# One set of tiles for both phases of a hybrid encoder layer: later weights split in the third block, first block's pooling done later, norm ahead of the fold

## The chip, the core and the metric

The kernel runs on one core of a Trainium2 chip, whose engines are named as in the profile: PE multiplies matrices (PEld loads its stationary operand), DVE and ACT do the work on vectors, POOL does a little arithmetic and issues the stores, and SP issues the loads. The metric is the device time of one execution in microseconds (us), from launch to end.

## The reference: what is computed

One encoder layer is applied to two groups, 512 and 2048 tokens of 1024 channels, with the same weights, in f32. Cut to what matters:

```
h = rmsnorm(x, norm_pre)
pool_u, pool_g, q, k, v, attn_g, merge = split(h @ w_in)        # w_in: 1024 x 6656
pooled = mean of pool_u over 2, 4, 8 or 16 neighbours - pool_u  # by channel group
pb = (pooled by group @ w_pool_group) * pool_scale * silu(pool_g)
ab = windowed_attention(rope(q), rope(k), v, sink) * silu(attn_g)
m = sigmoid(merge_p) * (pb @ w_pool_proj) + sigmoid(merge_a) * (ab @ w_attn_proj)
y = x + rmsnorm(m @ w_out, norm_post)
```

Attention sees a band of 128 tokens to either side; 16 heads share 4 heads of keys and values.

## The kernel before, in words

**Precision.** Each f32 operand is split into a high and a low part (`hi_lo`: a copy to the reduced format on ACT, a subtraction on DVE), and a product is three matmuls (`mm3`): high by high, high by low, low by high. So every weight that PE uses costs ACT one copy and DVE one subtraction, unless it was split before and lies split in memory.

**Phase 1** computes the input projection, for tokens in three blocks (768, 896 and 896 tokens), with all the normed tokens of a block held in `arena` as seven operands (B11, T2, B21, T1, T3, B22, T4). The 26 pairs of weight units of a block go through a scheme of seven products (M1, M6, M2, M5, M7, M3, M4, in this order) in place of eight; the sums of weights that it needs (S1 to S4) are formed in the first block (`sums`) and kept in memory for the other two. After its products a pair is finished on DVE and ACT by a `Post`: rotary embedding (`Rope`), gates (`Gate`, `Silu`), values transposed on PE (`Values.tr_steps`), or pooling (`Pool`: running sums over neighbours, a gate, the result stored as `pb`). The two halves U2 and U4 that a pair keeps until M7 and M4 lie in tiles `u`.

The pooling's group weights are folded into its part of the input projection first (`fold`: 32 steps of six matmuls, in items of four steps; an item loads three pieces of weights, `w_pool_group` and two of `wu_t`, into tiles with tag `u`, and splits them). Ahead of the first block the sums of squares of its tokens are taken (`stats_sum`), turned into the norm's factor, spread over the partitions by PE (`prep_r`, tile `rbc`), and the seven operands are formed (`first_operands`), on DVE above all.

Extra work is put beside the products by `hooks[(block, pair, step)]`: the next block's statistics, norm and operands, and the transposes of the values. One block's pairs 0 and 1, and its last two, run interleaved.

**Phase 2** goes over five blocks of 512 tokens: `pp` (pooling branch by `w_pp`), attention in groups of 128 queries by four heads, `ap` (attention branch by `w_ap`), and `out_phase` (by `w_out`, the second norm, the residual). A grid of slots sets which steps of attention stand between which steps of `pp` and `ap`. Here `wsplit` loads a piece of weights at its first use, splits it and stores it split; later uses load it split. `out_phase` has two halves of 512 channels with four accumulators each; when one is full, `evac` squares it on ACT, multiplies it by the norm's gain on DVE, and in the second half scales and adds.

**What sets the order.** PE's order is that of the code. Each other engine's order is set by the framework's scheduler when the program is built; an engine works in that order and waits at each instruction. Tiles with one tag share a fixed number of buffers (`z` 6, `u` 4, `w` 7, `R` 3); an instruction that writes a new tile waits until an old one is no longer read, and a tile that is stored is free when the store has landed. Phase 1 and phase 2 take their own tiles from two pools, `p1` and `p2`, of which the second is opened when the first is closed. `run` loads weights ahead of the steps by 7 tiles in phase 1 and by 5 in phase 2.

## Time and profile before

| | us |
|---|---|
| median of 3 runs | 2493.63 (2488.38 to 2495.53) |
| the profiled execution | 2490.91 |
| its span, first to last instruction | 2489.1 |
| PE busy in it | 2340.3 |
| DVE busy | 1775.7 |
| ACT busy | 1158.1 |

Reading it: the profiled execution lies 2.7 us below the median, and 1.8 us of it lie outside the span. PE's matmuls overlap each other in the trace, so that its busy time says when it was not idle. The granted clock of PE is 1.00 at 2.4 GHz and 0.50 at 1.2 GHz; a mean between them says how much of a stretch was spent at each.

### The profile page before, as it was taken

How to read it: one execution, taken by the hardware profiler on the slowest of the kernel's cores; microseconds unless marked ns; L12 is line 12 of the kernel's file. 1: busy time of each engine (PE TensorE's matmuls, PEld its weight loads, DVE VectorE, ACT ScalarE, POOL GpSimd, SP SyncE). 2: the span in 40 equal slices, each digit the busy share in tenths (PEclk: the TensorE clock that was granted, in tenths of full speed). 3: DMA queues.
4: the chain of work that ended last, by engine and by line, in shares of the span. 5: the costliest groups of instructions: out<-in, count | busy, mean ns of one | idle time of the engine just before them, and what ended most of it. 6: DMA issues, size and time to landing. Idle time of an engine off the chain costs nothing.

```text
span 2489.1 us, 34194 instructions
## 1 busy us (share of the span) xinstructions
PE 2340.3 (94%) x11668; PEld 2074.6 (83%) x11668; DVE 1775.7 (71%) x3370; ACT 1158.1 (47%) x2477; POOL 418.8 (17%) x897
## 2 busy tenths in 40 slices
PE   4799999989999999899999969999999999999998
PEld 4799999978898989798988858778788788878877
DVE  4888889866667777656667658887689488578632
ACT  5444433544443335333333446765466366456411
POOL 2332222112102110301011011112110110011011
PEclk8899999999999999999999989999999999999999
DMA  7676667665556647534444397889778787877774
GB/s 276 201 254 214 219 250 256 206 236 196 177 184 224 250 157 261 207 134 170 156 156 170 120 342 264 273 288 339 260 252 259 277 271 250 285 236 241 275 266 165
DMA packets 180847, 573.55 MB, mean 230 GB/s; under 512 B 25280, under 2 KB 32704, under 8 KB 170688
## 3 DMA queue, kind: packets, MB, share of 16 engines
q1 hardware_dynamic: 139408, 397.00, 48.0%
q0 software_dynamic: 41264, 174.36, 18.3%
q8 instruction: 92, 1.51, 0.2%
q14 instruction: 83, 0.68, 0.1%
HBM read 396.94 MB, written 174.33 MB: 230 GB/s over the span
## 4 chain that ended last, share of the span: by engine, by line
PE 57%; DVE 9%; DMA 6%; issue 4%; ACT 3%; POOL 1%; POOLq 0%; SPq 0%; ACTq 0%; DVEq 0%
PE ps_s L115 8%; PE ps_s L117 8%; PE ps_s L116 8%; PE ps_g L115 7%; PE ps_g L116 7%; PE ps_g L117 7%; PE ps_t L928 3%; PE ps_o L941 2%; DVE ps_s L904 1%; PE ps_o L940 1%; PE ps_s L900 1%; PE ps_s L901 1%; DMA h<-t 1%; DMA h<-ab 1%; DVE pt L85 1%
## 5 line engine op out<-in xcount | busy, mean ns | idle before, releaser
L115 PE MATMUL ps_s<-arena,w 128*128 128x448 f32 (+1 forms) x1512 | 547.4, 362 | 36.0 <-DVE u L381 20.7
L117 PE MATMUL ps_s<-arena,w 128*128 128x448 f32 (+1 forms) x1512 | 542.3, 359 | 0.0
L116 PE MATMUL ps_s<-arena,w 128*128 128x448 f32 (+1 forms) x1512 | 542.3, 359 | 0.0
L115 PE MATMUL ps_g<-arena,w 128*128 128x512 f32 (+2 forms) x1264 | 493.8, 391 | 22.7 <-ACT w L84 11.5
L116 PE MATMUL ps_g<-arena,w 128*128 128x512 f32 (+2 forms) x1264 | 479.9, 380 | 1.0 <-DVE arena L85 0.9
L117 PE MATMUL ps_g<-arena,w 128*128 128x512 f32 (+2 forms) x1264 | 478.6, 379 | 0.0
L84 ACT CAST w<-Q 128x512 fp32r<-128x512 f32 x312 | 192.8, 621 | 391.2 <-PE ps_s L117 335.4
L115 PEld LDWEIGHTS ps_s<-arena,w 128*128 128x128 f32 x1512 | 286.7, 190 | 63.2 <-DVE u L381 28.5
L117 PEld LDWEIGHTS ps_s<-arena,w 128*128 128x128 f32 x1512 | 286.4, 189 | 17.0 <-DVE w L85 0.4
L116 PEld LDWEIGHTS ps_s<-arena,w 128*128 128x128 f32 x1512 | 286.6, 190 | 16.1
L115 PEld LDWEIGHTS ps_g<-arena,w 128*128 128x128 f32 x1264 | 240.7, 190 | 44.6 <-ACT w L84 11.9
L117 PEld LDWEIGHTS ps_g<-arena,w 128*128 128x128 f32 x1264 | 240.6, 190 | 35.9 <-DVE w L85 0.2
L116 PEld LDWEIGHTS ps_g<-arena,w 128*128 128x128 f32 x1264 | 241.2, 191 | 21.9 <-DVE arena L85 2.0
L85 DVE TENSOR_TENSOR w<-Q,w 128x512 fp32r<-128x512 f32 x312 | 214.0, 688 | 31.3 <-ACT w L84 20.7
L906 ACT ACTIVATE P<-ps_s,nm 128x384 f32<-128x384 f32 (+1 forms) x320 | 179.6, 562 | 105.5 <-DVE nm L904 103.1
L85 DVE TENSOR_TENSOR w<-R,w 128x512 fp32r<-128x512 f32 x234 | 160.6, 687 | 86.7 <-ACT w L84 84.0
L84 ACT CAST w<-R 128x512 fp32r<-128x512 f32 x234 | 145.1, 621 | 139.3 <-PE ps_s L117 116.4
L904 DVE CUSTOM_DVE_ANT_0 ps_s<-ps_s,mask,nsink 128x384 f32<-128x384 f32 (+1 forms) x320 | 188.7, 593 | 14.6 <-PE ps_s L901 12.5
L85 DVE TENSOR_TENSOR pt<-ps_t,pt 128x512 fp32r<-128x512 f32 x224 | 153.6, 687 | 13.7 <-ACT pt L84 11.2
L84 ACT CAST pt<-ps_t 128x512 fp32r<-128x512 f32 x224 | 130.3, 583 | 53.0 <-PE ps_t L928 51.6
L928 PE MATMUL ps_t<-ident,P 128*128 128x128 f32 x896 | 141.0, 277 | 13.4 <-DVE P L915 7.3
L361 DVE TENSOR_TENSOR z<-ps_s,u 128x448 f32<-128x448 f32 (+1 forms) x144 | 86.3, 600 | 86.7 <-PE ps_s L117 82.7
(196 smaller groups left out, 3651.0 us busy)
## 6 DMA issues: line engine op xcount, KB each, us to landing
Q<-sw SPq DMA_DIRECT2D x52, 1024.0 KB, 5.1
R<-in_w_h SPq DMA_DIRECT2D x54, 768.0 KB, 6.1
w<-swpw_pp SPq DMA_DIRECT2D x64, 512.0 KB, 4.4
w<-swpw_ap SPq DMA_DIRECT2D x64, 512.0 KB, 4.5
w<-swpw_out SPq DMA_DIRECT2D x56, 512.0 KB, 4.6
sw<-Q POOLq DMA_DIRECT2D x26, 1024.0 KB, 6.3
z<-in_x SPq DMA_DIRECT2D x40, 512.0 KB, 6.0
arena<-q SPq DMA_DIRECT2D x20, 1024.0 KB, 7.5
```

The lines of the kernel that those rows point to most:

```text
L84: A.copy(hi, src)
L85: V.tensor_sub(lo, src, hi.bitcast(F32))
L115: T.matmul(o, lhsT=xs[0], rhs=ys[0], start=start, stop=False, skip_group_check=more)
L116: T.matmul(o, lhsT=xs[0], rhs=ys[1], start=False, stop=False, skip_group_check=more)
L117: T.matmul(o, lhsT=xs[1], rhs=ys[0], start=False, stop=stop, skip_group_check=more)
L361: V.tensor_add(dst, acc[:, c], t[:, c])
L900: T.matmul(s, lhsT=q, rhs=st["kh"][:, kc], start=True, stop=False)
L901: T.matmul(s, lhsT=q, rhs=st["kl"][:, kc], start=False, stop=True)
L904: V.tensor_tensor_reduce(s, s, mask[:, kb0 * 128:kb1 * 128], -1.0, nsink[:, H:H + 1], ALU.add, ALU.min, nm[:, h:h + 1])
L906: A.activation(P[:, 0:nk], s, AF.Exp, bias=nm[:, h:h + 1], scale=-1.0, accum_out=l[:, h:h + 1])
L928: T.transpose(tp[:, h * 128:(h + 1) * 128], pr[h][:, i * 128:(i + 1) * 128], cst["ident"])
L941: T.matmul(o, lhsT=v, rhs=pts[i][:, 1, :], start=False, stop=i == kb1 - kb0 - 1)
```

## The change

- **One set of tiles.** The pools `p1` and `p2` are gone. Phase 2 takes the tiles of phase 1 under their tags: its gates the `u` tiles, the attention's probabilities an `R` tile for four heads, their transposes a `Q` tile for two, the norm's gain the `A21` tiles, `out_phase`'s products the `rope`, `rbc` and `s` tiles. The squares are written to that product's tile rather than to one of their own. Both phases are one program, `run(phase1() + phase2(), 7)`. The two operand sets of phase 2 change places in `arena`.
- **Later weights.** All 48 pieces of `w_pp`, `w_ap` and `w_out` are loaded, split and stored in the third block of phase 1, 24 times 1024 columns, at hooks beside its pairs. Phase 2 loads them split only.
- **First block's pooling.** In the first block `Pool.finish` stores the two raw tiles (`rawu`, `rawg`). Eight hooks, four in the second and four in the third block, load them again (`again`) and pool (`later`).
- **Norm ahead of the fold.** The six squares stand together at the start, the norm's factor is taken at once (`rstd`), and `prep_r` follows 4 steps of the fold in place of 16; the operands' other parts follow 8 steps. Five of the eight items of the fold now stand between the first two pairs' products, where three stood.
- **Smaller moves.** The four steps that transpose the values stand wider apart; the next block's statistics and norm come some pairs earlier; in `out_phase` the last two pieces of weights are taken accumulator by accumulator; the first attention group follows 24 steps of `pp` in place of 9, and its loads are issued after 8.

```diff
-TILES_H, TILES = 7, 5
+TILES = 7
...
+    def utile():
+        return sb.tile([128, 512], F32, tag="u", bufs=4, name="u")
...
-    def prep_r(p1, s):
+    def rstd(s):
         t0, t1 = BLOCKS[s][0] // 128, BLOCKS[s][1] // 128
         n, ssq = t1 - t0, ssqs[s]
         G.tensor_scalar(ssq[:, 0:n], ssq[:, 0:n], 1.0 / D, EPS, op0=ALU.mult, op1=ALU.add)
         G.tensor_tensor(rcol[:, t0:t1], ssq[:, 0:n], mhalf[:, 0:n], ALU.pow)
-        rbc[s] = p1.tile([128, 896], F32, tag="rbc", bufs=1, name="rbc")
+
+    def prep_r(s):
+        t0, t1 = BLOCKS[s][0] // 128, BLOCKS[s][1] // 128
+        rbc[s] = row_tile()
...
+            if s > 0:
+                self.silu()
+                V.tensor_copy(gcarry[:, f, :], g[:, W:W + 8])
+                self.pool()
+                return
...
+            store(rawu[f], u[:, 0:n])
+            store(rawg[f], g[:, 8:8 + W])
+
+        def again(self):
+            self.z = [ztile(), ztile()]
+            nc.sync.dma_start(self.z[0][:, 0:self.n], rawu[self.f])
+            nc.sync.dma_start(self.z[1][:, 8:8 + self.W], rawg[self.f])
+
+        def later(self):
+            self.silu()
+            self.pool()
...
         def first():
...
-            xs = stats_load(0, range(3))
+            stats_sum(0, range(n0), stats_load(0, range(n0)))
+            rstd(0)
             fold0.load()
-            xs += stats_load(0, range(3, n0))
-            stats_sum(0, range(n0), xs)
             next(forming)
+            pairs[0].raw()
+            next(forming)
+            pairs[1].raw()
...
+        def beside(s, i, load, form, j=0):
+            box = {}
+            hook(s, i, j, lambda: box.update(x=load()))
+            hook(s, i, j + 3, lambda: form(box["x"]))
...
-            for j, f in enumerate(posts[NPAIR * s + 1].tr_steps()):
-                hook(s, 2, 2 + j, f)
+            for (i, j), f in zip(((2, 2), (2, 4), (3, 0), (3, 3)), posts[NPAIR * s + 1].tr_steps()):
+                hook(s, i, j, f)
...
+        first_pools = [x for x in posts[:NPAIR] if isinstance(x, Pool)]
+        for x, (s, i) in zip(first_pools, ((1, 14), (1, 15), (1, 20), (1, 22), (2, 5), (2, 7), (2, 11), (2, 13))):
+            beside(s, i, x.again, lambda _, x=x: x.later())
+        places = [i for i in range(2, NPAIR - 2) if i not in (5, 7, 11, 13)]
+        places = sorted((places + places)[:24])
+        for u in range(24):
+            i = places[u]
+            beside(2, i, lambda u=u: split_load(u), lambda x: split_form(*x), 2 if u and places[u - 1] == i else 0)
...
         prog.append((None, first))
-        prog += fs[0:16]
+        prog += fs[0:4]
         prog.append((None, second))
-        prog += fs[16:20]
+        prog += fs[4:8]
         prog.append((None, third))
-        fs = fs[20:]
+        prog += fs[8:12]
+        fs = fs[12:]
...
+    def split_form(z, dsts):
+        hi, lo = ztile(F32R), z.bitcast(F32R)
+        hi_lo(hi, lo, z)
+        for j, d in enumerate(dsts):
+            for e, t in enumerate((hi, lo)):
+                store(d[:, e, :], t[:, j * 512:(j + 1) * 512])
...
-    SETS = [(region(o, 8, 512), region(o + 4096, 8, 512)) for o in (0, 8192)]
+    SETS = [(region(o, 8, 512), region(o + 4096, 8, 512)) for o in (8192, 0)]
...
-        def wsplit(key, src):
-
+        def weights(key):
             w = wtile()
-            if key in swp:
-                move(w, swp[key])
-                return w
-            raw = p2.tile([128, 512], F32, tag="wr", bufs=3, name="wr")
-            nc.sync.dma_start(raw, src)
-            hi_lo(w[:, 0, :], w[:, 1, :], raw)
-            swp[key] = scratch("swp" + key, [128, 2, 512])
-            store(swp[key], w)
+            move(w, swp[key])
             return w
...
-                A.activation(junk, acc, AF.Square, accum_out=so[:, i:i + 1])
-                o = p2.tile([128, 512], F32, tag="og", bufs=4, name="og")
-                V.tensor_mul(o, acc, cst["gpost"][:, half * 512:(half + 1) * 512])
+                A.activation(o, acc, AF.Square, accum_out=so[:, i:i + 1])
+                V.tensor_mul(o, acc, cst["gpost"][half])
...
-                order = [(u, t) for t in range(4) for u in range(NKT)] if late else [(u, t) for u in range(NKT) for t in range(4)]
+                lead = 0 if late else NKT - 2
+                order = [(u, t) for u in range(lead) for t in range(4)] + [(u, t) for t in range(4) for u in range(lead, NKT)]
...
-                prog += first[:9]
-                fill = at(first[9:], pp_puts(1, 0)) + at(pp(1, 0), ap_puts(0, 1), PUTS0) + ap(0, 1, 0)
+                prog += first[:8] + [(None, lambda: fetch_kv(0, 0))] + first[8:24]
+                fill = at(first[24:], pp_puts(1, 0)) + at(pp(1, 0), ap_puts(0, 1), PUTS0) + ap(0, 1, 0)
...
-        with tc.tile_pool(name="p1", bufs=1) as p1:
-            run(phase1(p1), TILES_H)
-        with tc.tile_pool(name="p2", bufs=1) as p2:
-            run(phase2(p2), TILES)
+        run(phase1() + phase2(), TILES)
```

ACT's order at the start: of before, the part around the spread of the norm's factor (`rbc`); `h` are the fold's results, `w<-R` the first pairs' weights.

```order
L84 CAST w<-R 128x512
L211 COPY rbc<-ps_t 128x512
L211 COPY rbc<-ps_t 128x256
L84 CAST w<-R 128x512
L171 COPY h<-ps_t 128x512
L84 CAST arena<-z 128x384 x2
L171 COPY h<-ps_t 128x512
```

And of the change, from ACT's first work on; `w<-u` are the fold's weights, `arena` the first block's operands.

```order
L222 ACTIVATE z,ssq<-z 128x1024 x6
L105 CAST w<-u 128x512 x3
L197 COPY h<-ps_t 128x512 x2
L240 COPY rbc<-ps_t 128x512
L240 COPY rbc<-ps_t 128x256
L105 CAST arena<-z 128x384 x4
L105 CAST arena<-R 128x384 x4
L105 CAST arena<-z 128x384 x4
L105 CAST w<-u 128x512 x4
```

The factor is spread after one item of the fold rather than after four, and the weights of the fold's second item are now split behind twelve copies of operands.

DVE's order beside the first two pairs: of before, the last item of the fold (`raw`) and the two U4 halves (`u`), with buffer numbers.

```order
L85 TENSOR_TENSOR w_721<-raw_719,w_721 128x512
L85 TENSOR_TENSOR w_726<-raw_724,w_726 128x512
L85 TENSOR_TENSOR w_731<-raw_729,w_731 128x512
...
L389 TENSOR_TENSOR u_839<-ps_s_643,s_555 128x384
...
L389 TENSOR_TENSOR u_856<-ps_s_658,s_570 128x384
```

And of the change; `z_797` and `z_812` are the sums behind M7, which are the last to read the U4 halves `u_889` and `u_903`.

```order
L419 TENSOR_TENSOR u_903<-ps_s_702,s_614 128x384
L391 TENSOR_TENSOR z_797<-ps_s_968,u_889 128x384
L391 TENSOR_TENSOR z_812<-ps_o_985,u_903 128x384
L106 TENSOR_TENSOR w_949<-u_947,w_949 128x512
L106 TENSOR_TENSOR w_954<-u_952,w_954 128x512
L106 TENSOR_TENSOR w_959<-u_957,w_959 128x512
```

The fold's last item stood ahead of the U4 halves and now stands behind M7's sums; its three loads use the buffers of `u_889`, `u_903` and, once more, of `u_889`.

SP's order at the boundary of the phases: of before, from the first loads of attention on (`q`, `k`, `v`); `wr` is the first piece of `w_pp`, still to be split.

```order
L75 DMA arena<-q_114 128x4x512
L75 DMA arena<-k 64x512 x4
L696 DMA mask<-in_mask 128x384
L701 DMA gpost<-in_norm_post 128x1024
L75 DMA arena<-v 128x512
L717 DMA wr<-in_w_pp 128x512 x3
```

And of the change; `w<-w_pp` are pieces that are split already.

```order
L96 DMA w<-w_pp_0_137 128x1024
L828 DMA h<-pb_211 128x512
L96 DMA w<-w_pp_1_138 128x1024
L823 DMA u<-gp_201 128x512
L96 DMA w<-w_pp_0_139 128x1024
L966 DMA z<-sl_185 128x512
L96 DMA w<-w_pp_1_140 128x1024
L96 DMA arena<-q_131 128x4x512
L96 DMA w<-w_pp_0_141 128x1024
```

Four pieces of weights now stand ahead of attention's first load, where all of them stood behind it.

DVE's order at the end of `out_phase`: of before, from the first half's last products to the second half's (`og`; the sums `z<-og,ss,z` need the norm's factor `ss`).

```order
L812 TENSOR_TENSOR og<-ps_t,gpost 128x512 x2
...
L826 SCALAR_TENSOR_TENSOR z<-og,ss,z 128x512 x2
L812 TENSOR_TENSOR og<-ps_g,gpost 128x512 x2
L826 SCALAR_TENSOR_TENSOR z<-og,ss,z 128x512 x2
```

And of the change.

```order
L901 TENSOR_TENSOR s<-ps_g,A_12662 128x512
L915 SCALAR_TENSOR_TENSOR z<-rope,ss,z 128x512
L915 SCALAR_TENSOR_TENSOR z<-s,ss,z 128x512
L901 TENSOR_TENSOR s<-ps_g,A_12662 128x512
```

The product that frees the first accumulator `ps_g` stood behind two sums that wait for the norm's factor, and now stands ahead of them.

## Rows read from the trace of the kernel before

**Rows 1.** Page, busy time of each engine (share of the span), instructions.

```profile
PE 2340.3 (94%) x11668; PEld 2074.6 (83%) x11668; DVE 1775.7 (71%) x3370; ACT 1158.1 (47%) x2477; POOL 418.8 (17%) x897
```

**Rows 2.** Windows: length; PE, PEld, DVE, ACT, POOL busy; clock, DMA share, GB/s.

```profile
0.00:124.50 124.50, 77.41 (x439) 72.58 (x439) 85.91 (x146) 63.53 (x119) 35.83 (x59) 0.88 0.68 239
124.50:503.00 378.50, 358.74 (x2001) 353.28 (x1999) 319.82 (x542) 168.04 (x297) 95.21 (x198) 0.99 0.66 234
580.00:970.00 390.00, 384.35 (x1884) 352.56 (x1883) 275.05 (x417) 165.50 (x280) 51.12 (x97) 1.00 0.58 204
1046.00:1426.00 380.00, 376.31 (x1839) 344.47 (x1839) 252.13 (x383) 148.54 (x245) 46.61 (x93) 1.00 0.43 151
1426.00:1500.00 74.00, 50.89 (x224) 40.84 (x223) 38.71 (x96) 35.19 (x88) 14.15 (x30) 0.84 0.94 338
1500.00:1757.00 257.00, 247.47 (x1219) 202.75 (x1218) 206.57 (x504) 161.62 (x423) 51.53 (x119) 0.99 0.84 286
```

**Rows 3.** PE's waits: for whom, us in total, times, longest us.

```profile
PE ps_t L115 <- ACT w L84: 39.8, 6, 17.3
PE ps_s L115 <- DVE u L381: 20.7, 17, 2.9
PE ps_t L497 <- DVE z L85: 11.9, 5, 2.7
...
PE ps_g L115 <- DVE og L812: 9.8, 4, 2.5
```

**Rows 4.** Timeline of the start: start, us, instruction [idle before <-releaser].

```profile
42.93 0.86 ACT L211 COPY rbc<-ps_t 128x512 f32<-128x512 f32 x2
...
66.89 0.33 SPq L151 DMA_DIRECT2D raw<-in_w_pool_group  x1
...
69.63 0.62 ACT L84 CAST w<-raw 128x512 fp32r<-128x512 f32 x1
...
71.52 0.58 PE L115 MATMUL ps_t<-w 128*128 128x256 f32 x1 [17.27 <-ACT w L84]
```

**Rows 5.** Groups by shape, to 1430 us: busy us, mean ns | idle before.

```profile
L85 DVE TENSOR_TENSOR w<-Q,w 128x512 fp32r<-128x512 f32 x312 | 214.0, 688 | 31.3 <-ACT w L84 20.7
...
L551 DVE TENSOR_TENSOR z<-z 128x904 f32<-128x904 f32 x10 | 10.9, 1092 | 0.0
...
L85 DVE TENSOR_TENSOR arena<-z,arena 128x384 fp32r<-128x384 f32 x14 | 7.4, 550 | 0.7 <-ACT arena L84 0.7
...
L215 DVE SCALAR_TENSOR_TENSOR z<-z,gpre,rbc 128x768 f32<-128x768 f32 x6 | 6.0, 1012 | 0.0
```

**Rows 6.** Windows, columns as in rows 2: one item of the fold and more.

```profile
80.60:83.50 2.90, 2.90 (x26) 2.90 (x25) 2.85 (x8) 1.10 (x2) 0.31 (x1) 1.00 0.42 79
```

**Rows 7.** Timeline, PE behind a pooling of the first block.

```profile
392.72 0.69 PE L115 MATMUL ps_s<-arena,w 128*128 128x384 f32 x1 [2.89 <-DVE u L381]
```

**Rows 8.** Timeline: PE's transposes of values; windows: the clock after another.

```profile
546.37 0.88 PE L497 MATMUL ps_t<-ident,z 128*128 128x128 f32 x3 [2.72 <-DVE z L85]
...
1020.50:1027.20 6.70, 6.12 (x18) 5.30 (x17) 2.45 (x6) 1.64 (x4) 1.43 (x2) 0.50 0.59 196
```

**Rows 9.** Timeline at the boundary of the phases.

```profile
1433.81 2.29 SPq L717 DMA_DIRECT2D wr<-in_w_pp  x3
...
1441.05 0.80 PE L115 MATMUL ps_g<-arena,w 128*128 128x512 f32 x1 [11.47 <-ACT w L84]
```

**Rows 10.** Timeline at the end of `out_phase`; windows: the clock after it.

```profile
1752.86 1.27 DVE L812 TENSOR_TENSOR og<-ps_g,gpost 128x512 f32<-128x512 f32 x2
...
1753.59 0.50 PE L115 MATMUL ps_g<-arena,w 128*128 128x512 f32 x1 [2.47 <-DVE og L812]
...
1754.40:1757.70 3.30, 3.30 (x9) 2.61 (x8) 3.30 (x6) 0.00 (x0) 1.16 (x2) 0.50 0.43 171
```

**Rows 11.** Timeline: ACT and then PE, second block's start.

```profile
567.63 0.94 ACT L84 CAST z<-z 128x896 fp32r<-128x896 f32 x1 [4.42 <-DMA v<-z]
...
573.71 0.74 PE L115 MATMUL ps_s<-arena,w 128*128 128x448 f32 x1 [3.02 <-DVE u L389]
```

More of the change, by code (lines that the diff above doesn't have):

```diff
@@ L142, in run, with fold @@
             f()
-    def fold(p1):
+    def fold():
         steps = []
         def raw_split(src):
-            raw = p1.tile([128, 512], F32, tag="u", bufs=4, name="raw")
+            raw = utile()
             nc.sync.dma_start(raw, src)
@@ L319, in raw @@
                 return
-            self.R = self.p1.tile([128, 1536], F32, tag="R", bufs=NR, name="R")
+            self.R = rtile()
             for c0, c1, src in self.srcs:
@@ L387, in f @@
                 elif r == "M5":
-                    st["U4"] = pair.p1.tile([128, 512], F32, tag="u", bufs=4, name="u")[:, 0:w]
+                    st["U4"] = utile()[:, 0:w]
                     V.tensor_add(st["U4"], acc, st["s"])
@@ L725, in unit @@
             for half in range(2):
-                it = Item(lambda half=half: wsplit(f"{name}{u}_{half}", a[name][u][:, half * 512:(half + 1) * 512]))
+                it = Item(lambda half=half: weights((name, u, half)))
                 for i in range(4):
@@ L837, in make @@
                 def make(u, half=half, late=late):
[L838 removed]
+                    key = "w_out", half, u
                     if not late:
[L840 removed]
+                        return weights(key)
                     w = SETS[1 - mt]
```

149 lines of the change are left out of this document (96 added, 53 removed).

## The prediction, written before the changed kernel was timed

> **What bounds the kernel now.** I read the page first: PE is busy for 2340 us of 2489, DVE for 71%, ACT for half [rows 1]. PE's work stays the same, instruction for instruction, so only PE's 149 us of idle time and the time that it spends at half its clock can be won. Next the windows, cut by stage [rows 2]: the start is idle for 47 us of 124.5 at a mean clock of 0.88; the first block for 19.8 of 378.5; the second and third, behind their first pairs, for only 5.7 and 3.7; the boundary of the phases for 23.1 of 74 at 0.84; the first part of phase 2 for 9.5 of 257. Then PE's waits [rows 3], which name causes: 39.8 us for the fold's weights, 20.7 for U2 (`u L381`), 11.9 for DVE at the transposes of values, 9.8 at the first accumulator behind `out_phase`. In the windows a wait of some 2.5 us or more is followed by a stretch at clock 0.50: 3.3 us of busy PE at half rate, which at full rate had taken half, so 1.7 us on top of the wait [rows 10]; after the transposes of the third block 6.7 us [rows 8].
>
> **The change, part by part.** The sum is made against the profiled execution's 2490.9 us; the median is 2.7 above it.
>
> *End of `out_phase`.* DVE frees `ps_g` at the end of two products at 1752.86, behind sums that wait for the norm, and PE starts at 1753.59 after 2.47 us [rows 10]. In the new order that product stands first. The first accumulator is also full earlier: the last two pieces go accumulator by accumulator, six matmuls each, so three accumulators, 18 matmuls of about 0.2 us (1219 in 247 us [rows 2]), follow the first: 3.7 us in which ACT's square and DVE's product (0.6 to 0.7 us each, the second now behind the first since they write one tile) are hidden. If that cover went, the old 2.5 us would return. Four waits of 2.45 us go [rows 3], and the half-rate stretches behind three of them, 1.7 us each (one is in [rows 10]): **minus 15**.
>
> *The boundary.* SP issues the first `w_pp` at 1433.8, behind attention's loads, and PE stands for 11.5 us until ACT has split it [rows 9]. Afterwards four split pieces stand ahead of the first load of attention; they need neither ACT nor DVE, and the operand set 1, now in B11, T2 and B21, is free after M2, with 96 matmuls of 0.2 us still to come, 19 us before phase 1 ends. The load of `q` still blocks SP, but only until M3 of the last pair has been read; the four pieces give PE 48 matmuls, 10 us, and the keys, values and later pieces have 24 steps (72 matmuls, 15 us) to land where 9 steps stood. Of the stage 23.1 us are idle; a clock of 0.84 makes 24 of 74 us at half rate, and if half of them were busy, 6 more are lost [rows 2]. Of these 29 I leave 3: **minus 26**. Bounds: minus 13 (only the 11.5 and its clock) to minus 29.
>
> *Transposes of values.* A step needs a PSUM tile that DVE must have emptied; with two steps apart in place of one, DVE has 5 us. All 11.9 us of waits [rows 3] and some 6 us of half rate behind them (the longest stretch costs 3.1, half of 6.12 [rows 8]) could go, 18. But the third and fourth step now fall where the pair before finishes a `Rope`, and the values hold two `z` tiles longer: **minus 14**, bounds minus 18 to 0.
>
> *First block's pooling.* A pooling is 4 to 7 instructions of DVE of about 1 us [rows 5] (776 columns in the first block, so 0.97 as an estimate between 768 and 904), 44 us for eight. They leave the first block, where DVE is busy for 84%, and make it 73%. At 71% the second block idles 5.7 us of 390 [rows 2]; so the first should fall from 19.8 to about 8: **minus 12**. The wait of 2.89 us behind such a pooling is one of them [rows 7].
>
> *What the other blocks get.* The second block gets four short poolings, 18 us: DVE 71 to 75%, **plus 3**. The third gets 26 us of poolings and the splits: 48 times 0.688 us, 33 us [rows 5], as 24 instructions of twice the length (estimate 1.3 us). DVE goes from 66% to 82%. Near 84% the first block lost 20 us; but it also formed sums there, which the third does not: from 3.7 to 15, **plus 11**. ACT's 48 copies of 0.62 us [rows 4], 30 us, lie beside 148 of 380, POOL's 96 more stores beside 47 of 380 [rows 2]. Bounds: 0, if all of it fits between PE's needs, to 39, if each of 32 insertions costs the usual wait for `u L381`, 1.2 us (20.7 over 17 [rows 3]).
>
> *Phase 2's first part.* The same 33 us of DVE leave it, from 80 to 67%; of its 9.5 us of idle time 2.5 are `out_phase`'s: **minus 4**, bounds minus 7 to 0.
>
> *The start.* The factor `rbc` is ready at 43.8 us, the fold's sixth item runs at 71.52 after 17.3 us of waiting [rows 4]. Now six loads of 0.5 MB come first, at 239 GB/s [rows 2] 13 us; with 8 us for the factor, one item at half rate and the copies, `rbc` is there at about 21. But in between DVE has 58 instructions to do before the fold's fourth item: 8 norms of 1.01, 16 of 512 columns of 0.69, 34 of 384 of 0.55 [rows 5], 38 us, and ACT splits the fold's second item only behind twelve copies that follow those norms. So the fourth item runs at 59, 12 us earlier, with two items fewer done: 48 matmuls, 5.4 us [rows 6]. Net minus 7. Against it stands the eighth item. Its first two loads need the buffers of the U4 halves, so they wait for M7's sums, and its third needs the first's: load to copy takes 2.7 us [rows 4], twice, with 1.3 for split and subtraction between; PE has only this item ahead. That is 6 us, plus 1.7 at half rate. **Plus or minus 0**, bounds minus 7 to plus 10.
>
> The prefetch by 7 tiles of 7 makes SP wait for PE one piece longer; behind it stand the loads of gates and operands, needed 8 steps (24 matmuls, 5 us) later: nothing, and at worst what little of those loads sticks out of 5 us. The pools' boundary itself costs only what the boundary's term holds.
>
> Sum: -15 - 26 - 14 - 12 + 3 + 11 - 4 + 0 = -57, so 2434 on the profile's scale; with the median somewhat above it I say 2435.
>
> **A rule weighed.** In the third block the DMA engines are busy for 0.43 of the time at 151 GB/s, in the first part of phase 2 for 0.84, with PE busy for 96% [rows 2]. The moved weights and tiles add some 42 MB in 380 us, 110 GB/s, and bring 0.43 to about 0.74, below a share that PE has been seen to bear. The Trainium skill, page "Trainium Kernel Development and Optimization", section Key Constraints, says that the DMAs of all issuing engines run on the same 16 engines and interleave; by that the third block's loads and stores all get slower with the new traffic, which speaks against the move. The trace agrees that the engines are shared: at a share of 0.84 PE still waits little, so by the row it costs nothing, and by the rule alone, transfers longer by two thirds, it would feed the rival below.
>
> **The rivals.**
> - *Slower: `z` tiles run out in the third block.* A split holds two of the six `z` tiles until its four stores have landed, a pooling up to four. That ACT waits 4.4 us for a store of a `z` tile and PE then 3.0 us does occur [rows 11]; with 1.7 at half rate 4.7 us. Were it so at each of 32 insertions, it costs 150 in place of 11: 2574. It decides from 2.5 us per insertion (57 + 11 + 8 over 32) on. Against it: pairs of the third block hold no operands being formed, and a pooling now takes two working tiles, not up to five.
> - *The insertions cost a usual wait each*, 39 in place of 11: 2463.
> - *The boundary only changes its wait*: the split pieces wait behind `q` and the operands behind DVE's last sums, 13 of 26 stay: 2448. This is also the case in which the one set of tiles does not do its work.
> - *The start gains*: the eighth item's stall is covered and DVE forms sooner, 12 to 15 us: 2421.
>
> **How the numbers follow.** Chances: the forecast 0.62, its own range 2412 to 2456 (the bounds of boundary and transposes at one end, of the start and the insertions in part at the other); insertions dear 0.13; boundary 0.08; start 0.11; slower 0.06. The range 2402 to 2472 takes in all but the slower case and the tails of the others. What a measurement of this kernel can tell from no change is about 0.3%, 7.5 us, so 2486 to 2501 is "same": the upper tail of the dear insertions and the near end of the slower case, 0.03; slower 0.04; faster 0.93.
>
> **What would show it.** Right: no wait of PE for `ps_g` behind `out_phase`; PE crosses the boundary with under 5 us idle; DVE near 73% in the first block and 82% in the third; the eighth item of the fold waits some 6 us behind M7. Wrong: ACT or DVE waiting for stores of `z` tiles at many pairs of the third block, or PE idle for over 20 us there; PE still waiting 10 us at the boundary; a start whose fourth item runs much later than 59 us.

## The result: 2.6% slower, and where the time went

The changed kernel takes 2554.64 us (median of 4 runs, 2552.34 to 2564.07) against 2491.88 for the kernel before; the ratio is 1.0259 (95% interval 1.0228 to 1.029). The profiled execution has a span of 2562.3 us, 73.2 more than that of before, and lies 9.4 us above its own median; the sums below are made against these two spans, so some 10 us of them belong to that execution and not to the change.

The page's busy times of the changed kernel, to be held against [rows 1]:

```profile
PE 2361.5 (92%) x11668; PEld 2099.0 (82%) x11668; DVE 1778.3 (69%) x3346; ACT 1156.8 (45%) x2461; POOL 446.3 (17%) x961
```

PE has the same 11668 matmuls and hardly more busy time: the loss is idle time and clock. The windows by stage, columns as in [rows 2]: the start, the first block, the second and third from pair 2 on (pairs are counted from 0), the boundary up to the 96th matmul of phase 2's projections, the first part of phase 2. They begin and end by work done and so not at the places of [rows 2], whose windows of the second and third block begin behind pair 3.

```profile
0.00:112.20 112.20, 69.22 (x366) 65.32 (x367) 69.15 (x120) 57.34 (x107) 26.85 (x41) 0.82 0.64 232
112.20:494.20 382.00, 364.53 (x2036) 361.35 (x2036) 300.09 (x514) 167.09 (x302) 86.80 (x163) 0.98 0.72 250
529.00:989.60 460.60, 428.01 (x2038) 388.73 (x2037) 319.10 (x479) 182.13 (x307) 80.26 (x166) 0.97 0.57 200
1025.30:1517.60 492.30, 429.89 (x2030) 390.11 (x2029) 332.11 (x484) 191.53 (x305) 128.52 (x262) 0.94 0.65 229
1517.60:1547.50 29.90, 27.65 (x122) 22.43 (x122) 8.48 (x24) 7.37 (x20) 2.75 (x7) 0.94 1.03 377
1547.50:1822.70 275.20, 260.83 (x1296) 215.94 (x1295) 206.19 (x520) 161.36 (x435) 29.41 (x88) 0.98 0.77 254
```

The kernel before, second and third block between the same pairs:

```profile
530.40:964.50 434.10, 419.77 (x2038) 383.46 (x2037) 303.85 (x458) 179.47 (x304) 70.87 (x134) 0.99 0.57 202
999.30:1429.20 429.90, 417.98 (x2030) 381.25 (x2030) 283.79 (x429) 166.26 (x276) 68.30 (x134) 0.99 0.46 159
```

In the third block PE is idle for 62.4 us at a clock of 0.94, where before it was idle for 11.9 at 0.99; the second idles 32.6 in place of 14.3. The boundary idles 2.3 us; before, it took 60.3 us up to the same projection matmul and idled 20.3. PE's waits, columns as in [rows 3]:

```profile
PE ps_s L141 <- DVE z L391: 74.1, 17, 17.2
PE ps_t L141 <- ACT w L105: 41.2, 7, 13.9
PE ps_s L141 <- DVE u L411: 28.4, 14, 4.7
PE ps_t L1019 <- DVE Q L106: 19.5, 8, 5.0
```

The same two waits in the kernel before, where attention's transposes are called `pt`:

```profile
PE ps_s L115 <- DVE z L361: 7.3, 5, 2.9
PE ps_t L928 <- DVE pt L85: 5.9, 6, 2.8
```

The first line has grown tenfold: 17 waits of up to 17.2 us for DVE's sum into a pair's `z` tile (L391). The 9.8 us for `og` [rows 3] are gone; the waits for attention's transposes (`Q`) went from 5.9 to 19.5 us.

Since PE's order is the same but for small moves, both traces can be divided by work done: at the first matmul of each pair in phase 1, and at equal counts of projection matmuls in phase 2. The differences of those stretches (after less before, us) add up to the 73:

| stretch | after less before |
|---|---|
| start, pairs 0 and 1 of the first block | +3.2 |
| first block: pairs 2 and 3; the others | +13.0; -15.8 |
| second block: pairs 2 and 3; the others | +5.7; +20.8 |
| third block: pairs 2 and 3; 4, 6, 9, 15, 22; the other pairs | +28.9; +32.4; +1.2 |
| pairs 0 and 1 of the second and third block | -0.9 |
| boundary and first part of phase 2 | -16.5 |
| five output parts and the stretch ahead of the last; the three stretches of attention between the other four | -11.9; +13.2 |

What happens at a bad pair shows in the timeline of the third block's pair 2 (start, us, instruction, idle before and what ended it):

```profile
1043.71 0.78 POOL L99 DMA_DIRECT2D v<-z  x1 [4.19 <-DVE z L106]
1050.20 0.73 POOL L99 DMA_DIRECT2D v<-z  x1 [5.71 <-issue]
1052.78 1.04 ACT L105 CAST z<-z 128x1024 fp32r<-128x1024 f32 x1 [9.23 <-DMA v<-z]
1053.86 1.23 DVE L106 TENSOR_TENSOR z<-z 128x1024 fp32r<-128x1024 f32 x1 [9.85 <-ACT z L105]
1054.14 2.33 POOL L99 DMA_DIRECT2D w_pp<-z  x4 [3.21 <-ACT z L105]
1057.55 0.62 DVE L391 TENSOR_TENSOR z<-ps_s,u 128x448 f32<-128x448 f32 x1 [2.46 <-DMA w_pp<-z]
...
1058.23 0.74 PE L141 MATMUL ps_s<-arena,w 128*128 128x448 f32 x1 [17.22 <-DVE z L391]
```

Read from the bottom: PE waits for DVE's sum; DVE stood for 9.85 us at a split's subtraction, behind ACT's copy of that split (1024 columns, so it can be nothing else); ACT stood for 9.23 us because the copy's new `z` tile still held values `v`, whose store was issued only at 1050.20, behind the landing of the store of values ahead of it at 1049.8 (the last section returns to this). Everything behind them in the two queues, PE's own needs among it, stood too. ACT's waits of this kind in the third block (for whom, us, times, longest), which before came to 7.7 us there:

```profile
ACT z L105 <- DMA v<-z: 16.5, 3, 9.2
ACT z L105 <- DMA q<-z: 9.8, 2, 6.2
ACT z L105 <- DMA sl<-z: 6.8, 2, 4.9
...
ACT z L105 <- DMA pb<-z: 5.0, 1, 5.0
ACT z L105 <- DMA w_pp<-z: 4.9, 1, 4.9
```

### The profile page after: what moved, and what is told of

It is laid out like the page before. It is cut to its first block, busy times and chain, and to the rows that moved or that the text cites. A ratio compares the mean times of both kernels' runs of the same rounds, so it can differ in the third digit from the quotient of the medians.

```text
span 2562.3 us, 34370 instructions
## 1 busy us (share of the span) xinstructions
PE 2361.5 (92%) x11668; PEld 2099.0 (82%) x11668; DVE 1778.3 (69%) x3346; ACT 1156.8 (45%) x2461; POOL 446.3 (17%) x961
## 4 chain that ended last, share of the span: by engine, by line
PE 42%; DMA 8%; DVE 8%; issue 3%; ACT 2%; POOL 1%; SPq 0%; POOLq 0%; DVEq 0%; ACTq 0%
PE ps_g L141 6%; PE ps_g L143 6%; PE ps_g L142 6%; PE ps_s L141 4%; PE ps_s L142 4%; PE ps_s L143 4%; PE ps_t L1019 3%; PE ps_o L1034 2%; PE ps_o L1033 2%; PE ps_s L991 1%; PE ps_s L992 1%; DVE ps_s L995 1%; DVE Q L106 1%; DMA h<-ab 1%; DMA ab<-z 1%
## 5 line engine op out<-in xcount | busy, mean ns | idle before, releaser
L141 PE MATMUL ps_s<-arena,w 128*128 128x448 f32 (+1 forms) x1512 | 556.5, 368 | 112.5 <-DVE z L391 74.1
L142 PE MATMUL ps_s<-arena,w 128*128 128x448 f32 (+1 forms) x1512 | 550.6, 364 | 0.0
L143 PE MATMUL ps_s<-arena,w 128*128 128x448 f32 (+1 forms) x1512 | 549.8, 364 | 0.0
L141 PEld LDWEIGHTS ps_s<-arena,w 128*128 128x128 f32 x1512 | 291.6, 193 | 143.0 <-DVE z L391 81.0
L143 PEld LDWEIGHTS ps_s<-arena,w 128*128 128x128 f32 x1512 | 292.2, 193 | 17.5
L142 PEld LDWEIGHTS ps_s<-arena,w 128*128 128x128 f32 x1512 | 291.9, 193 | 16.8
L997 ACT ACTIVATE R<-ps_s,nm 128x384 f32<-128x384 f32 (+1 forms) x320 | 179.5, 562 | 147.3 <-DVE nm L995 139.8
L106 DVE TENSOR_TENSOR Q<-ps_t,Q 128x512 fp32r<-128x512 f32 x224 | 153.5, 686 | 14.1 <-ACT Q L105 11.7
L1019 PE MATMUL ps_t<-ident,R 128*128 128x128 f32 x896 | 139.9, 278 | 22.9 <-DVE Q L106 19.5
L391 DVE TENSOR_TENSOR z<-ps_s,u 128x448 f32<-128x448 f32 (+1 forms) x144 | 86.2, 598 | 100.8 <-PE ps_s L143 95.3
L1019 PEld LDWEIGHTS ps_t<-ident,R 128*128 128x128 f32 x896 | 111.8, 142 | 49.9 <-DVE Q L106 22.1
```

Source lines behind the costliest of these rows:

```text
L106: V.tensor_sub(lo, src, hi.bitcast(F32))
L141: T.matmul(o, lhsT=xs[0], rhs=ys[0], start=start, stop=False, skip_group_check=more)
L142: T.matmul(o, lhsT=xs[0], rhs=ys[1], start=False, stop=False, skip_group_check=more)
L143: T.matmul(o, lhsT=xs[1], rhs=ys[0], start=False, stop=stop, skip_group_check=more)
L391: V.tensor_add(dst, acc[:, c], t[:, c])
L997: A.activation(P[:, 0:nk], s, AF.Exp, bias=nm[:, h:h + 1], scale=-1.0, accum_out=l[:, h:h + 1])
```

## Experiments

Each was timed beside the kernel before. "Above before" is the difference of the same stretch in the traces, as in the table. A trace is one execution, up to 9 us from its kernel's median, so a few us in one stretch can be chance: pairs 0 and 1 of the third block lie between 0.5 below and 6.6 above before, though no run's edit is there.

### One: parts undone or moved

**splits_h**: the third block's splits in other tiles.

```diff
-        z = ztile()
+        z = [htile(), htile()]
...
-        hi, lo = ztile(F32R), z.bitcast(F32R)
+            hi, lo = half_tile(F32R), t.bitcast(F32R)
```

> The changed kernel with the split of the later weights in other tiles: the raw halves in the four h tiles, which stand free in the third block, the rounded halves in the two A21 tiles. The same values are computed, in 48 copies and subtractions of 512 columns in place of 24 of 1024. Theory (the z tiles run out): behind its first two pairs the third block took 62.5 us longer than before the change, of which pairs 4, 6, 9, 15 and 22 hold 5.7, 5.1, 10.0, 3.8 and 7.8, 32 in all, and pairs 2 and 3 29. Without the z tiles of the splits the 32 go and of the 29 about half, so 45 us less: 2510, and no wait of ACT for a store of a z tile at those pairs. Rival (the work of the splits itself fills the queues of ACT and DVE): the instructions stay, so the third block stays within 10 us: 2545 to 2560.

Measured: 2554.89 us, ratio 1.0241 (1.0224 to 1.0259). Pairs 4, 9, 15 and 22 lost their excess as the theory said, but pairs 5 to 8 and 11 to 13 (without 9 and 10) now lay 3.0 to 9.2 us above before each, and the third block still 56. That is the rival's number. Its waits of ACT point to another cause than work, though:

```profile
ACT A L105 <- DMA h<-in_w_ap: 15.2, 3, 9.9
ACT A L105 <- DMA w_pp<-A: 15.0, 3, 9.2
ACT A L105 <- DMA h<-in_w_out: 13.6, 3, 7.8
```

The new tiles had run out as well: four splits were loaded ahead of pair 2 and the last at pair 12, where the code has them at pairs 2 to 23. So no split stood at pairs 15 and 22 any more, and that their excess went says nothing about tiles. The last group of experiments takes this up.

**values_old**, **stats_pair4**, **pools_first**: the three other things that were moved in phase 1.

```diff
-zip(((2, 2), (2, 4), (3, 0), (3, 3)), ...tr_steps())
+zip(((2, 2), (2, 3), (2, 4), (2, 5)), ...tr_steps())     # values_old
-zip((3, 5, 7, 9), range(t0, t1, 2))
+zip((4, 5, 7, 9), range(t0, t1, 2))                      # stats_pair4
-            if s > 0:
+            if True:                                     # pools_first: Pool.finish, and no hooks
```

> The changed kernel with the four steps that transpose the values back in the second pair, at its steps 2, 3, 4 and 5, as before the change. Theory (the values hold two z tiles into the third pair, where the queries' rotation, which takes six, and the loads for the norm ask for them too): the third pair of blocks 0 and 1, 10.5 and 10.6 us longer than before, falls back by about 10 each, the second pair of block 1 gets its 4.9 us back, and the third block's pairs 2 and 3 lose some 10 of their 29: 2525 to 2535. Rival (the loads for the norm at the third pair are what is short, or the splits): no change in the third pair, and 5 us more in the second pair of each block: 2555 to 2570.

> The changed kernel with one edit: the first two rows of the later block's norm are loaded beside pair 4 and not beside pair 3. Theory (z tiles asked for by the rotation, the values and these loads at once): pair 3 of blocks 0 and 1 gets 3 to 7 us back each, the third block, which has no such loads, stays: 2540 to 2549. Rival (the respaced transposes alone are the cause): within 3 us of 2555.

> The changed kernel with the eight poolings of the first block back at the end of their own pairs in the first block (no storing and loading of raw results); the rest as changed. Theory (z tiles): in block 1 the pairs 15 to 22, 17.5 us longer than before, lose about 12 of them; the first block's pairs 15 and 19 get back their 4.5 us each and the others 3 more, 12 in all; the third block's poolings, at pairs 5, 7, 11 and 13, cost nothing and give nothing: 2550 to 2560. Rival (the third block's loss comes from DVE's load, of which the poolings are 26 us): the third block falls by 20 or more: 2535 or less.

Measured: values_old 2552.53 (ratio 1.0236, 1.0217 to 1.0255), which the expectation missed. In the second block pairs 2 and 3 fell from 5.7 to 3.1 above before, in the first they rose from 13.0 to 18.5. stats_pair4: 2547.84 (1.0217, 1.0189 to 1.0245); pairs 2 and 3 fell from 13.0 to 6.1 (pairs 4 and 5 took back 5.7 of it) and from 5.7 to -0.4, the third block hardly moved. So the loads for the norm beside pair 3 are a part of the loss there, and neither edit alone frees the pair. pools_first: 2568.78 (1.0294, 1.0272 to 1.0316), above the 2550 to 2560 expected: in the second block pairs 15, 21 and 22 lost 14.1 us, as expected; the first block got 29 longer, more than the 12 expected, above all at pairs 11, 13, 17 and 19, which follow a pooling and now also form operands; the third block fell by only 7.5. The poolings there are not the larger part of its loss.

The expectation called the second block's loss one of `z` tiles. The changed kernel's timeline at pair 15 does not show that:

```profile
796.65 1.02 DVE L595 SCALAR_TENSOR_TENSOR z<-z,pscale 128x768 f32<-128x768 f32 x1
797.70 0.97 DVE L610 TENSOR_TENSOR z<-z 128x776 f32<-128x776 f32 x1
798.58 0.62 DVE L391 TENSOR_TENSOR z<-ps_s,u 128x448 f32<-128x448 f32 x1
...
799.25 0.74 PE L141 MATMUL ps_s<-arena,w 128*128 128x448 f32 x1 [4.04 <-DVE z L391]
```

DVE works through two instructions of a moved pooling (768 and 776 columns) ahead of the sum that PE waits for. At these three pairs DVE waits for no store, and ACT for 0.3 us at most; PE waits 1.9 and 4.0, 4.3, and 2.4 us for DVE.

**splits_apart**, **splits_back**: the same splits at other places.

```diff
-        places = sorted((places + places)[:24])
+        places = sorted([*range(2, NPAIR - 2), 16, 20])      # splits_apart
...
+            raw = sb.tile([128, 512], F32, tag="wr", bufs=2, name="wr")   # splits_back, in weights()
+            nc.sync.dma_start(raw, src)
+            hi_lo(w[:, 0, :], w[:, 1, :], raw)
+            store(swp[key], w)
```

> The changed kernel with the 24 splits of the third block one to a pair (pairs 2 to 23, two at 16 and 20) in place of two each at pairs 2, 3, 4, 6, 8 and 9; they use z tiles as in the changed kernel. Theory (a second split within two steps asks for z tiles whose stores have not landed): pairs 4, 6 and 9, 5.7, 5.1 and 10.0 us above before, lose nearly all of that, pairs 2 and 3 some 8 of 29, pairs 15 and 22 keep their 11.6, pairs 5, 7, 11 and 13, which now hold a pooling and a split, gain up to 2 each: 2530 to 2540. Rival (each insertion costs its own wait wherever it stands): the third block stays within 8 us: 2547 to 2560.

> The changed kernel with the splits of the later weights out of the third block and back at their first use in phase 2 (two raw tiles for that, and six split weight tiles in place of seven, fetched six ahead in place of seven). Theory (splits and respaced transposes share the third block's loss): the third block behind its first pairs falls from 62.5 us above before to 12 to 20, which is pairs 2 and 3 with the transposes; the first part of phase 2 gets 4 to 12 back: 2510 to 2525. Rival (the poolings and transposes make the loss without the splits): third block still 40 or more above before: 2540 or more.

Measured: splits_apart 2558.49 (1.0272, 1.0251 to 1.0294), against the expectation: pairs 2, 3, 6 and 9 lost 32.2 of their excess, but pairs 5, 7, 11 and 13, a split beside a pooling, got 7.6 to 9.4 longer. At those four pairs PE waits 5.8 to 7.0 us at once for DVE's sum, while ACT waits for no store there and DVE for 2.7 us at most: there a pooling and a split stand in DVE's queue together. What counts is not the number of splits alone but what stands beside them: in the changed kernel the excess stands behind a rotation (pairs 3, 9, 15) or a pooling (6, 22), and hardly any in pairs 8, 10, 12, 14 and 16 to 21, of which pair 8 has two splits. splits_back: 2532.98 (1.017, 1.0148 to 1.0191), slower than expected; the third block lies 3.1 above before, so the splits hold 59 of its 62.5, but boundary and first part of phase 2 took back 20, where 4 to 12 were expected. Its third block behind the first pairs, columns as in [rows 2]:

```profile
1035.60:1468.60 433.00, 419.94 (x2030) 383.99 (x2029) 309.29 (x466) 171.67 (x286) 78.00 (x167) 0.98 0.50 172
```

### Two: phase 2

**cut_30**, **row3_h**.

```diff
-CUTS = (28, 46, 64)
+CUTS = (30, 46, 64)                                          # cut_30
-                xs = ztile()
+                    xs = [htile(), htile()]                  # row3_h, if t == 3
```

> The changed kernel with the first part of phase 2 taking 30 groups of attention and not 28. Theory (24 steps of the first projection now stand ahead of attention, so the operand loads of the next projection, which are placed by steps of the projection, come earlier against attention's outputs than before the change, and SP and ACT wait for their stores): from projection matmul 96 to 576 the time per matmul falls, ACT's wait of 5.2 us for the load of such an operand goes, and the four stretches of attention together lose 5 to 9: 2545 to 2550. Rival (what is lost there is the denser mix of attention itself): no gain, 2552 to 2560.

> The changed kernel with the fourth row of x in each output part in two h tiles, one for each half, in place of a z tile. Theory (that row's load waits until the first row's store has freed a z tile, DVE's product of it stands ahead of attention's masks, and PE waits 5.1, 4.1 and 3.8 us for it behind the output parts): these three waits go, with the half-rate stretches behind them, 10 to 17 us: 2538 to 2545. Rival (the wait moves: the row stands behind the next weights on SP's queue, or DVE is late for another reason): within 4 us of 2555.

Measured: cut_30 2554.45 (1.0259, 1.0235 to 1.0282): nothing, its theory falls. row3_h 2541.19 (1.0214, 1.0186 to 1.0242): the three stretches behind the output parts fell from 13.2 above before to 6.3 below. What it took away, in the changed kernel's timeline:

```profile
1828.13 0.33 SPq L910 DMA_DIRECT2D z<-in_x  x1
...
1833.98 0.75 DVE L915 SCALAR_TENSOR_TENSOR z<-rbc,ss,z 128x512 f32<-128x512 f32 x1 [4.85 <-DMA z<-in_x]
...
1836.45 0.48 PE L1019 MATMUL ps_t<-ident,R 128*128 128x128 f32 x1 [5.05 <-DVE Q L106]
```

The output part ends without a wait at 1822.7, PE takes up attention, and 9 us later stands for 5.05 us for DVE, which waits for the fourth row of `x`: its `z` tile came free late, as SP's wait ahead of that load shows.

```profile
SPq L910 <- DMA out_prompt<-z: 4.9, 1, 4.9
```

**before_og6**, **before_lead**: was it the order that removed the waits of [rows 10]?

```diff
-                o = p2.tile([128, 512], F32, tag="og", bufs=4, name="og")
+                o = p2.tile([128, 512], F32, tag="og", bufs=6, name="og")    # before_og6
+                lead = 0 if late else NKT - 2                                # before_lead: the new order
```

> The kernel before the change with six tiles in place of four for the output part's products. Theory (the four products of the first half hold all four tiles until the norm's sums have read them, so the second half's first product, which frees the accumulator, stands behind those sums): the four waits of 2.5 us of TensorE for the output's product and the half-rate stretches behind them go, 8 to 15 us: 2477 to 2484. Rival (it is the order of the matmuls): the waits stay, within 4 us of before.

> The kernel before the change with the new order of the output part alone: the last two weight pieces run accumulator by accumulator. Theory (tiles): the accumulator is full earlier but its product still waits for a tile; with 18 matmuls or 3.7 us behind it that wait is covered in part, so up to 10 us are won: 2480 to 2491. Rival (the order is what counts, as forecast): the four waits go, 2474 to 2480. If both kernels lose the waits, either edit alone is enough.

Measured: before_og6 2497.85 (1.0026, 1.0014 to 1.0038), before_lead 2495.62 (1.0011, 0.9999 to 1.0023). Either edit alone takes all four waits away, and neither gains: PE's waits behind the output parts, of the first and of the second kernel, where before had 9.8 for `og` and 2.3 for `ps_o`:

```profile
PE ps_o L941 <- DVE pt L85: 17.9, 4, 6.0
```

```profile
PE ps_o L942 <- DVE pt L85: 13.3, 4, 4.6
```

The next wait takes the place: in the first kernel the fourth row of `x` again (DVE waits 6.15 us for it). Removing only the wait that shows is worth nothing here.

### Three: the tiles freed, and the splits held in place

**mended** joins what the runs pointed to; **mended_tr**, **mended_order** and **mended_back** take one thing out of it.

```diff
+        places = [(1, i) for i in (6, 8, 10, 12, 14, 15, 16, 18, 20)]
+        places += [(2, i) for i in (4, 6, 8, 9, 10, 12, *range(14, 23))]
...
+            if s > 0 or f not in (2, 3, 4, 5):          # poolings 2 to 5 go to (2, 5), (2, 7), (2, 11), (2, 13)
...
+            hook(s, i, j + gap, ...)                     # gap 4 for splits and operands
+            zip(((2, 1), (2, 3), (2, 5), (2, 6)), ...tr_steps()), vt = htile(F32R)
```

> The changed kernel with what the runs so far point to: the splits in h and A21 tiles, one to a pair, nine in the second block and fifteen in the third, none beside a pooling, formed four steps behind their load; only the four poolings of pairs 10, 12, 16 and 18 moved, to the third block's pairs 5, 7, 11 and 13; the norm's rows from pair 4 on; the operands formed four steps behind their load; the transposes of the values at steps 1, 3, 5 and 6 of pair 2, into h tiles; the fourth row of x in h tiles. Theory (all losses against before are waits for tiles that others hold, and go where the tiles are free): third block from 62 above before to under 8, second block from 26 to about 0, first block's pairs 2 and 3 from 13 to about 2, output parts with row 3 13 less: some 100 under the changed kernel, 2445 to 2465, faster than before. Rival (the moved work is too much for ACT and DVE wherever it stands): each of 24 splits still costs 2 us: 2490 or more.

> The mended kernel with the values as before the change: steps 2, 3, 4 and 5 of pair 2, into z tiles. The spaced steps were forecast to be worth 14 us. Theory (spacing helps when the tiles are there): 8 to 15 above the mended kernel. Rival (the spacing gives nothing even then): within 4 of it.

> The mended kernel with the order of the output part as before the change (all accumulators advance together to the end). The new order was forecast to be worth 15 us. Theory (with the fourth row out of the way its worth shows): 8 to 15 above the mended kernel, and waits of 2.5 us for the output's product behind four parts. Rival (PE waits there for another reason and the order gives nothing): within 4 of it.

> The mended kernel with the splits back at their first use in phase 2 (two raw tiles, six split weight tiles, fetched six ahead). Theory (the first part of phase 2 paid some 20 us for them, the second and third block now pay little): 12 to 20 above the mended kernel. Rival (the splits cost as much wherever they stand): within 5 of it.

Measured: mended 2492.28 (0.9997, 0.9983 to 1.0012), short of its theory; mended_tr 2509.68 (1.0065, 1.0045 to 1.0085), 17 more, but in it the scheduler also loaded four splits of the third block ahead of its pair 2, where mended loaded none, so the transposes alone are shown by the first block, which has no splits (pairs 2 and 3: 4.1 above before in place of 0.6 below); mended_order 2491.43 (1.0004, 0.9989 to 1.0018), no difference, and no wait for the output's product came back; mended_back 2466.4 (0.9898, 0.988 to 0.9916), *less* by 26. In mended_back the second block lies 9.5 and the third 7.9 below before, in mended 11.8 and 28.1 above: the splits still cost 57 us in h tiles, one to a pair as written. As run, all nine of the second block were loaded by its pair 7 and all fifteen of the third by pair 11. A bad place in mended:

```profile
1093.59 3.45 SPq L772 DMA_DIRECT2D h<-in_w_ap  x4
1097.36 1.28 ACT L105 CAST A<-h 128x512 fp32r<-128x512 f32 x2 [8.32 <-DMA h<-in_w_ap]
...
1099.29 0.74 PE L141 MATMUL ps_s<-arena,w 128*128 128x448 f32 x1 [6.44 <-DVE u L419]
```

Only PE's order is that of the code. The scheduler that orders the other queues puts a load that depends on nothing but a free tile ahead of its place, and the copies with it. SP's order of mended in the third block (`Q<-sw` comes once a pair, `h<-in_w_` are splits, two loads to a split; other loads are left out):

```
L772 DMA h<-in_w_ap 128x512 x4
L364 DMA Q<-sw_108 128x2048
...
L772 DMA h<-in_w_ap 128x512 x6
L364 DMA Q<-sw_112 128x2048
...
L772 DMA h<-in_w_out 128x512 x4
L364 DMA Q<-sw_125 128x2048
...
L772 DMA h<-in_w_out 128x512 x6
```

**splits_h_pinned**, **mended_pinned**: the same, with each split's load and copy held behind the instruction traced before it on its queue.

```diff
-            nc.sync.dma_start(t, x)
+            tc.keep_in_program_order(nc.sync.dma_start(t, x))
...
-            hi_lo(hi, lo, t)
+            tc.keep_in_program_order(A.copy(hi, t))
+            V.tensor_sub(lo, t, hi.bitcast(F32))
```

> The kernel of splits_h (raw halves in h, rounded halves in A21 tiles) with the loads and the copies of the splits pinned behind the instruction traced before them on their queue; nothing else is changed. Theory (the scheduler pulled the splits ahead, most of them into pairs 2 to 11, where they wait for each other's stores): pairs 5 to 8 and 11 to 13, 3 to 9 us each above before, lose most of that where one split stands in a pair; some stays at pairs 3, 4, 6, 8 and 9 with two: third block 15 to 35 above before in place of 56, in all 2515 to 2538. Rival (the work itself): third block 50 or more above before, 2550 or more.

> The mended kernel with the loads and copies of the splits pinned behind the instruction traced before them on their queue. Theory (placement): the 12 and 28 us that the second and third block lost in the mended kernel fall to minus 9 to plus 2 each, as in the kernel with the splits back in phase 2, while phase 2's first part keeps its 20: 2440 to 2456, the fastest so far. Rival (the work itself): 2480 or more.

Measured: splits_h_pinned 2518.56 (1.0099, 1.0075 to 1.0122), the third block 26.7 above before in place of 56. mended_pinned 2435.8 (0.9774, 0.9754 to 0.9794), 2.3% faster than before and the fastest kernel here. Its page, third block and boundary:

```profile
PE 2323.5 (95%) x11668; PEld 2070.6 (85%) x11668; DVE 1775.3 (73%) x3370; ACT 1156.0 (47%) x2481; POOL 446.5 (18%) x957
```

```profile
992.60:1415.50 422.90, 415.56 (x2031) 380.60 (x2030) 319.73 (x486) 184.53 (x311) 109.06 (x226) 1.00 0.66 237
1415.70:1443.60 27.90, 26.44 (x122) 21.22 (x121) 7.68 (x23) 6.78 (x20) 2.58 (x6) 1.00 1.03 394
```

Against the changed kernel's third block (492.3 us, DVE 332 and ACT 192 busy) DVE and ACT do nearly as much (nine of the splits stand in the second block, which is faster than before too), yet PE idles 7.3 us in place of 62.4. Against mended_back, which splits in phase 2, the pinned splits cost some 5 us in the second and third block and save 27 at the boundary and in the first part of phase 2.

## Why the prediction was wrong, by its own steps

- **Third block, plus 11: the step that failed.** It measured 62.5, of which 59 are the splits. The term was sized by DVE's share and by the usual wait for U2 (1.2 us), as if engine time were what is short, evenly over the block. At pairs 2, 3, 4 and 6 (39.7 us) tiles were short: a split held two of six `z` tiles from load to landed store, and the copy that waits for one stops ACT's and DVE's queues. At pairs 15 and 22 (11.6 us) no engine waits for a store; DVE does a pooling's or a rotation's and a split's instructions ahead of the sum that PE needs, and a mean share does not show that either. Pair 9 (10.0 us) has a load of a split that lands late (ACT waits 3.5 us) and a rotation ahead of the sum; how much of these three pairs goes back to tiles is not shown. The slower rival named the mechanism of the first four and got a chance of 0.06, on the argument that these pairs form no operands. But rotations (six `z` tiles each), gates and the values that wait for their transposes hold `z` tiles all the same, and these were never counted. The base was read too low as well: the window of [rows 2] begins at 1046 us, behind pairs 2 and 3, where 28.9 of the 62.5 arose; its 3.7 us of idle time are 11.9 from pair 2 on. The rival's price, 4.7 us at each of 32 insertions, was wrong the other way: most of the loss stood at seven pairs. Neither the prediction nor that rival saw a second thing, that the written place of a split binds nothing but PE; it matters little in the changed kernel, whose few `z` tiles kept the splits near their place, and decided between 2492 and 2436 in the mended ones.
- **Second block, plus 3:** pairs 4 and up came to 20.8. Four poolings cost 14.1 (pools_first), at pairs 15, 21 and 22: DVE's 18 us of work was counted in full, but not that two or more of its instructions at once stand ahead of a sum that PE needs. Pairs 11, 13, 17 and 19 cost 7.5, and 0 in the mended kernel; there operands are formed four steps behind their load in place of three, but the poolings had left too, so these 7.5 are not divided further.
- **Transposes of values, minus 14:** pairs 2 and 3 measured plus 13.0 and 5.7, and 4.0 in the third block without splits. The wider spacing carries the values into pair 3, where a rotation and the norm's loads want `z` tiles; the bounds, minus 18 to nothing, did not allow for a loss. With the transposes spaced inside pair 2 and in h tiles, as in the mended kernel, these two pairs of the three blocks lie 0.6, 8.6 and 6.0 below before: 15 us, the forecast's amount, but not by the spacing alone, since the norm's loads moved from pair 3 to pair 4, which now lies 2.8 and 6.0 above before in the first two blocks.
- **First block's pooling, minus 12:** minus 15.8. Right in amount; DVE's share fell from 86% to 79% between the same pairs, not to 73%.
- **End of `out_phase`, minus 15:** the waits went, 12.3 us with the clock behind the last of them, but the step did not ask what is late next: 13.2 us came back at the fourth row. With that out of the way (row3_h) ends and stretches together lie 18.6 below before. The cause was given too narrowly, too: tiles for the products do what the new order does, and in the mended kernels the order makes no difference (mended_order).
- **Boundary, minus 26, and first part of phase 2, minus 4:** minus 16.5 together (minus 20 to 25 in the eleven other kernels whose phase 2 is the same there, so this execution is the odd one). The crossing itself is as forecast (idle 2.3 us, forecast under 5); the first part brought no gain of its own (PE idle 14.4 us behind the boundary, 12.4 before).
- **Start, 0:** plus 3.2. The factor is spread at 20.1 to 21.2 us (forecast 21), the fold's fourth item runs at 58.06 (forecast 59), the eighth waits 4.1 us in a half-rate stretch (forecast 6).
- **SP's prefetch, nothing:** not tested by itself.
- **The rule weighed:** with the new traffic the third block's DMA share is 0.65 (forecast 0.74). Landings grew by 0 to 1.4 us: `Q<-sw` from 5.0 to 5.7, `sl<-z` from 4.9 to 6.0, `h<-pb` from 2.9 to 4.3, `v<-z` stayed at 2.5 (medians). Such growth alone does not make the loss; as the mended_pinned row shows, a share of 0.66 goes with PE busy for 98%. The Trainium skill, page "Trainium Kernel Development and Optimization", section Key Constraints, says that all DMAs share 16 engines; the longer landings agree with it.

In mended_pinned, where ACT waits for hardly any store, the whole is worth 55 us against the 57 forecast: the three blocks 15 (forecast 12), boundary and first part of phase 2 23 (30), output parts and attention between them 18 (15), the start 1 slower (0). The sum is close in part by luck, since its parts miss both ways and that kernel is not the one forecast: it moves four poolings in place of eight and takes other tiles for values, splits and the fourth row.

## What to carry to other kernels

Before work is moved beside other work, count the buffers that both hold from load to landed store, not only the engines' free time: an in-order queue turns one missing tile, or a bunch of moved instructions, into a wait for all that stand behind. Look in the built order where moved work really stands, since a hook's place in the code may bind one engine alone, and pin what has to stay. And where a wait is removed, ask what ends last next; here two edits each removed it in full and gained nothing.

## What the runs showed that was not expected

POOL stood for 5.71 us between two stores of values in the timeline above with nothing that the profile shows to end it (17.5 us over five such stores in the changed third block, 9.2 over three before). The landings show a pattern: in the kernel before, each of the 17 stores of values that directly follow another one is issued 0.30 to 0.45 us after that one's landing, while the three stores of another kind that follow one of values are issued 1.5 to 1.9 us before it. So stores of values go one at a time in these traces; what makes them do so was not tested. In the timeline above the first of the two landed after 6.06 us (median 2.5), at 1049.8, ahead of the next issue at 1050.20. While such a gap lasts, the `z` tile of the second store stays taken, so most of ACT's 9.23 us there is this gap, and not the number of tiles alone.
